# Sixteen-kilobyte rows instead of four: the expert weights of a mixture of experts, loaded one matrix at a time

## The chip, the cores and the metric

The kernel runs on one core of one Trainium2 chip. The metric is the device time of one execution in microseconds; the number of a kernel is the median of its runs. A separate execution is profiled, and its trace gives the times of single instructions and transfers.

## The reference

The computation is a small network of three layers on one sequence of 256 tokens with 1024 features, all in float32. The first two layers are a mix of a gated linear recurrence and a sparse attention; the third has an RWKV mixer beside a forgetting attention, and then a mixture of experts. Only the last part is touched here. It has 64 experts in 8 groups of 8. Each token goes to the best group, and in it to the two best experts. An expert has three matrices:

```
hid = jax.nn.silu(xblk @ w_gate[e]) * (xblk @ w_up[e])
return hid @ w_down[e]
```

Here w_gate and w_up are 1024 x 512 and w_down is 512 x 1024, so each is 2 MB, and the 64 experts hold 192 such matrices, 403 MB in all. With 256 tokens and two experts each, an expert sees few tokens, but its weights have to be read once all the same.

## The kernel before, in words

The three layers run one after the other. The weights of the first layers come through a small ring (raw, L241). The experts' weights are loaded on the SP queue into slots of 16 KB per partition, 2 MB each. There are ten at the end: some become free while the third layer's mixer still runs (L1120, L1312), the rest at its end (L1241, L1618). On the profile, some slots are called slot and three lie in the tile called arena; they take turns.

The experts run in 16 groups of four (this "group" of the kernel is half a group of the routing). For each group `experts` (L1540) does the following:

- It gathers the tokens' rows by a matmul with a selection matrix (L1534). Each expert has 32 rows, so that four experts fill 128.
- It multiplies with w_gate and w_up (L1566) into two accumulators, pg and pu. The four experts use four bands of 32 output rows (index j), and the 1024 features are summed over k = 0 to 7. A partition p holds the rows 8p to 8p+7 of an expert's matrix, so k is the row within a partition.
- Tanh on ScalarE (L1570) and two VectorE operations (L1571, L1572) make the hidden values, which PE transposes (L1576) and ScalarE copies (L1578).
- It multiplies with w_down (L1585, function `down`) into two accumulators, one for each half of the output columns, with k = 0 to 3.
- In `add` (L1588), ScalarE copies each half (L1590), a matmul weights it by the gates and puts it back in the order of the tokens (L1593), and VectorE adds it to x (L1595).

The matmuls are in float32. The trace has two matmul records for each matmul of L1566 and L1585.

`expert_load` (L1495) is the k-th of the 12 loads of a group. Loads 0 to 7 go in turn to w_gate and w_up: each takes two of the eight rows of a partition from all four experts. Loads 8 to 11 take one of the four rows of w_down from all four experts:

```
src = self.A[n][bass.ds(e0, 4)].rearrange("e (p k) f -> p e k f", k=8)[:, :, 2 * k:2 * k + 2]
```

Two rows of 512 floats lie next to each other in memory, and so does one row of 1024, so what is contiguous is 4 KB in either case, four times for each partition. Only the last group's w_down is loaded in another shape (L1501 to L1506): by halves of the columns, as two transfers for each load.

The order is set by the list `ahead` (L105) of all loads of all 16 groups. `fill` (L1515) issues the next load whenever a slot has no more readers to come in the program; `used` (L1520) says that some have been read. A load that is issued waits on the chip, on SP, until the matmuls that read its slot before have ended. What SP has behind it waits with it: later loads, and at the end the output (L1597). In `experts`, each load is given back on its own: after 16 matmul records for w_gate and w_up (eight matmuls), and also after 16 for w_down.

After the 16 groups there is a loop for experts with more than 32 rows (L1628). In the profiled execution it runs no time.

Of the kernel before, what the change touches and what calls it, by code (L numbers as in the profile page):

```python
# [11 lines left out]
OP = mybir.AluOpType  # L12
# [4 lines left out]
SLOT = 32          # rows of an expert in a pass  # L17
KEY = 512          # key of an assignment: expert * KEY + rank
# [4 lines left out]
# columns of the packed constants  # L23
# [3 lines left out]
# columns of the MoE's constants  # L27
M_KT, M_IO, M_OV, M_KG, M_END = 0, 128, 136, 144, 160
# columns of a hybrid layer's packed parameters
# [3 lines left out]
# columns of the third layer's packed parameters  # L33
# [3 lines left out]
ARENA = 24512      # floats of a partition in the one tile for what is float32 throughout  # L37
# [12 lines left out]
PAIRS = ((0, 1024, 3072), (7168, 5120, 4096))   # of a pair of chunks: where AR, M and BKt are  # L50
# [4 lines left out]
def run_all(steps):  # L55
    """Takes all steps; what they return."""
    while True:
        try:
            next(steps)
        except StopIteration as end:  # L60
            return end.value


def merged(a, b, every):
    """Steps of a, with one of b after every so many; what b returns."""
    n = 0
    for cost in a:
        yield cost
        n += 1
        if n % every == 0 and b is not None:  # L70
            try:
                yield next(b)
            except StopIteration as end:
                b, res = None, end.value
    if b is not None:
        res = yield from b
    return res


class Net:  # L80
    def __init__(self, ctx, tc, A, norm):
# [6 lines left out]
        self.holes = [(0, ARENA, 0)]        # offset, size, when freed  # L88
# [46 lines left out]
    # ---- on-chip memory: blocks whose tiles follow each other  # L135
# [9 lines left out]
    # ---- regions of one tile; Tile orders accesses to what overlaps  # L145
# [60 lines left out]
    def rot(self, shape, name, bufs=2, dt=F32, at=None):  # L206
        """The next of bufs buffers that take turns; freed by name like others."""
# [15 lines left out]
    # ---- float32 products in three passes: each operand is split exactly into two parts of 12 bits  # L223
# [8 lines left out]
    # ---- weights: blocks stream through a ring, in the order in which they are used  # L232
# [15 lines left out]
    def weights_steps(self, name, k, pin=False):  # L248
        """A weight block of k rows per partition, split."""
# [22 lines left out]
    def mm3_steps(self, out, lhs, rhs, first, last):  # L272
        """out += lhs^T rhs over lists of (hi, lo) pairs."""
# [13 lines left out]
    def rsqrt(self, out, v):  # L287
        """1 / sqrt(v) by Newton's steps, from an estimate by the exponent's bits."""
# [9 lines left out]
    # ---- h = rms_norm(x) g, rows moved to partitions (row 128 k + p), split; in steps as halves of x come  # L298
# [61 lines left out]
    def out_steps(self, yT, wo, then=None, tiles=(0, 1), half=0):  # L360
        """x += y wo, for halves of wo's rows from the given one on."""
# [25 lines left out]
    def log1p_half(self, e, z, z2, s):  # L387
        # s = log1p(e) / 2 = atanh(e / (2 + e)) for 0 <= e <= 1
# [11 lines left out]
    def hybrid_params(self):  # L400
        """Parameters of both hybrid layers; the decay constant -4 softplus(-lam)."""
# [14 lines left out]
    def chunk(self, name, pin=False):  # L416
        """A column block of an input projection: two halves of four k rows."""
        return run_all(self.chunk_steps(name, pin))
# [9 lines left out]
    def step(self, cols, pin=False):  # L428
        """Steps of the work that fills gaps, for about so many columns of the tensor engine."""
        self.pin = pin  # L430
        while cols > 0:
            n = next(self.side, None)
            if n is None:
                return
            cols -= n
# [16 lines left out]
    def hybrid(self, l, w0, then):  # L452
# [17 lines left out]
        # ---- q, k_s, k_w: token layout, norm, rotary; v_s, v_w  # L470
# [54 lines left out]
        # ---- compressed keys and values  # L525
# [7 lines left out]
        # partial sums over half of the rows each: keys at partitions 0 and 32, values at 64 and 96  # L533
        pcp = self.p("tp")
        Xs, cks = [], []
        for a in range(2):
# [11 lines left out]
            # token 16 n + 2 j + par  # L548
# [65 lines left out]
        # ---- compressed branch: scores of all heads, softmax, weights by gate  # L614
# [35 lines left out]
        # ---- selected and window branches: a head's three stages beside those of others  # L650
# [43 lines left out]
    def rg_part(self, l, hT, yT, sgn):  # L694
        """The recurrent half, in steps."""
# [17 lines left out]
        def silu(w, out):  # L713
            # without its factor 0.5
# [33 lines left out]
        # u = sqrt(1 - a^2) * i * x, with 1 - a^2 = tanh(-log a) (1 + a^2)  # L748
# [16 lines left out]
    def softmax(self, ps, mask, gate, at=None):  # L765
        """Weights of a head's scores [128 q, (q tile 0: 128 keys, q tile 1: 256)]."""
# [19 lines left out]
    def turned(self, P):  # L786
        """Keys moved to partitions."""
# [23 lines left out]
    def mixer(self, w0, more):  # L811
# [8 lines left out]
        # what the chunks' products read, by pairs of chunks: each pair's room becomes one slot of the experts' weights  # L820
        AR = [self.t([128, 4, 2, 2, 64], f"AR{i}", at=a[0]) for i, a in enumerate(PAIRS)]    # m, parity, (alpha, rho), t
        BK = self.t([128, 4, 2, 2, 2, 64], "BK")    # m, pair, parity, (kappa, beta) or (beta, kappa), s
        UV = self.t([128, 2, 2, 8, 64], "UV")       # v, and what the chunks add, with tokens on partitions
# [30 lines left out]
        # tanh of the decay rows; the rows of a stay as they are; sigmoid of the gate rows  # L854
# [17 lines left out]
        # log decay, its running sum within chunks of 64, P = exp of it  # L872
# [13 lines left out]
        # k: unit vectors kk (per head), k' = k (1 + (a - 1) k_a)  # L886
# [7 lines left out]
        def rest(w2):  # L894
            # r, v and the attention's q and k, between the steps of the inverse
# [66 lines left out]
        # a = 0.5 (1 + ta); beta = kk a / P; kappa = k' / P; alpha = -kk P_{t-1}; rho = r P  # L962
# [13 lines left out]
        # (I - B)^-1 for the strictly upper B[s, t] = beta_s . alpha_t: blocks of 1, 2, 4, 8, 16 merged within  # L976
        # blocks of 32, then those; partitions: even chunks at 64, odd ones at 0
        B = self.t([128, 2, 8, 64], "B", at=4608)
        BT, Q, BO = (self.t([128, 2, 8, 32], n, at=a) for n, a in (("BT", 10240), ("Q", 6656), ("BO", 10752)))
        TX = self.t([128, 2, 2, 8, 32], "TX", at=5632)      # the inverse and its transpose  # L980
# [96 lines left out]
        # products within chunks: rows (kappa, beta), columns (alpha, rho)  # L1077
# [15 lines left out]
        # the chunks in order: U = T (alpha S + A_ak V), Y = rho S + [A_rk A_rb] [V U], S = (S + [kappa beta] [V U]) P  # L1093
# [3 lines left out]
        # what the group norm multiplies and adds: weight, bonus and shift, each by the gate  # L1097
# [25 lines left out]
        def norm(i, y):  # L1123
            # group norm, bonus, gate
# [29 lines left out]
        def parts():  # L1154
            # of the output projection what the heads and the first tokens allow
# [14 lines left out]
        def other():  # L1170
            """Some of what is beside the chain."""
# [77 lines left out]
    def fox_gate(self, z):  # L1249
        T, V, S = self.T, self.V, self.S  # L1250
        c = self.c
        # -cumsum of log sigmoid(z), in three parts that bf16 carries exactly
# [5 lines left out]
        V.scalar_tensor_tensor(s, s, 2.0, e, OP.mult, OP.subtract)      # -log f  # L1258
# [20 lines left out]
    def fox_qk(self, hT, wi):  # L1279
        """q and k of the attention, to be taken in small steps between other work."""  # L1280
# [34 lines left out]
    def fox_heads(self, v, yT, more):  # L1315
        """The heads' attention in stages, a head's three beside those of others."""
# [35 lines left out]
    # ---- routing: top 1 of 8 groups, top 2 of its 8 experts  # L1352
    def route_init(self):
# [9 lines left out]
        self.oh = t([128, 2, 3, 8], "r_oh")             # tile; group, choices  # L1363
# [7 lines left out]
        self.key = t([128, 2, 2], "r_key")              # choice, tile  # L1371
# [7 lines left out]
    def route_step(self, tt, hf):  # L1379
        """Half a token tile of x is final."""  # L1380
# [14 lines left out]
        if hf:  # L1395
            if tt:
                # the first experts' rows among the first tile's, while the second tile is routed
# [4 lines left out]
    def route_tile(self, tt):  # L1402
# [16 lines left out]
        def first(vals, top, i):  # L1419
            # index - 128 and one-hot of the first of vals that equals top  # L1420
# [12 lines left out]
        # el holds the logits with their sign turned  # L1433
# [7 lines left out]
        # one-hot of both over the 64 experts; an assignment's rank among its expert's  # L1441
# [16 lines left out]
        # keys as group g of four experts sees them  # L1458
        V.tensor_tensor(self.keyg[:, :, :, tt], self.key[:, :, tt].unsqueeze(1).broadcast_to([128, 16, 2]),
                        self.cm[:, M_KG:M_KG + 16].unsqueeze(2).broadcast_to([128, 16, 2]), OP.subtract)  # L1460
        # the two choices' probabilities
# [10 lines left out]
    def route_more(self):  # L1472
        """Passes beyond the first: how many multiples of SLOT the fullest expert exceeds."""
# [9 lines left out]
    # ---- experts  # L1483
    first = None

    def moe_memory(self):
        """Room for what the routing and the experts need; the rest in slots for 2 MB of weights each."""
# [6 lines left out]

    def expert_load(self, g, k):  # L1495
        """The k-th of the 12 loads of four experts' weights."""
        e0, n, k = g * 4, "wd" if k > 7 else ("wg", "wu")[k % 2], k - 8 if k > 7 else k // 2
        w = self.slots[self.nslot % len(self.slots)]
        self.nslot += 1
        if n == "wd" and isinstance(g, int) and g == 15:  # L1500
            # the last: columns by halves  # L1501
# [5 lines left out]
        if n == "wd":  # L1507
            src = self.A[n][bass.ds(e0, 4)].rearrange("e (p k) d -> p e k d", k=4)[:, :, k:k + 1]
        else:
            src = self.A[n][bass.ds(e0, 4)].rearrange("e (p k) f -> p e k f", k=8)[:, :, 2 * k:2 * k + 2]  # L1510
# [4 lines left out]
    def fill(self):  # L1515
        """Loads of what is next into the slots that have no more readers to come."""
# [7 lines left out]
    def gather(self, key, kt):  # L1524
        """Rows of x for four experts, transposed, in a step for each token tile."""
# [14 lines left out]
    def experts(self, key, kt, out=None):  # L1540
        """Four experts: their rows of this pass gathered, run, and added into x by gate."""
# [19 lines left out]
        for k2 in range(0, 8, 2):  # L1561
            for dst in (pg, pu):
                w = self.early.pop(0)
                for k in (k2, k2 + 1):
                    for j in range(4):
# [250 lines left out]
```

## Time and profile before

| | us |
|---|---|
| median of three runs | 1565.11 |
| lowest and highest run | 1561.07, 1567.47 |
| span of the profiled execution | 1561.9 |
| PE busy | 1200.3 |
| VectorE busy | 545.6 |
| ScalarE busy | 309.1 |

The span goes from the first to the last instruction. PE's busy time counts matmuls whose ends are modelled and that overlap each other, so it is not a measure of PE at its peak. In the page's 40 slices a slice is 39 us; the digit is the busy share in tenths. The experts begin at about 600 us, slice 15. The line of DMA gives the mean share of the 16 DMA engines, and GB/s what they moved. A share may come out slightly above 1, as packets overlap a little at their ends. A "packet" of the page is what a DMA engine moves in one piece.

### The profile page before, as it was taken

To read this page: it belongs to the slowest core of one execution; us is meant where nothing else is said; L and a number is where in the kernel's file an instruction comes from. 1 tells how busy PE (TensorE), PEld (TensorE's weight loads), DVE (VectorE), ACT (ScalarE), POOL (GpSimd) and SP (SyncE) were. 2 spreads that over 40 slices of the span, in tenths; PEclk is the share of its full clock that TensorE was granted. 3 is DMA by queue.
4 is the path that set the end of the run, shared out by engine and by line. 5 is a ranking of instruction groups with operands and counts; after the bars stand their busy time and mean duration, and the time that the engine had idled before them with its cause. 6 is when DMAs were issued, how large, how long until landed. Compare 5 with 4: busy or idle time off the path is not lost.

```text
span 1561.9 us, 20735 instructions
## 1 busy us (share of the span) xinstructions
PE 1200.3 (77%) x8695; PEld 664.4 (43%) x8695; DVE 545.6 (35%) x1380; ACT 309.1 (20%) x733; POOL 170.9 (11%) x156
## 2 busy tenths in 40 slices
PE   6799989988889998887685775766766756758765
PEld 5767777767767674333132230331331312313311
DVE  6968786777665464111010110110101101101001
ACT  4556455644323221000000000000000000000000
POOL 3412431244232200000000000000000000000000
PEclk9999989998997798887788788997888989888888
DMA  7421532232311268999999999999999999999996
GB/s 273 161 96 41 213 128 97 79 140 92 111 57 54 108 250 343 409 409 410 409 409 409 410 409 409 410 409 409 409 409 409 409 409 409 409 409 409 409 408 254
DMA packets 113412, 464.94 MB, mean 298 GB/s; under 512 B 4236, under 2 KB 4364, under 8 KB 107428
## 3 DMA queue, kind: packets, MB, share of 16 engines
q1 hardware_dynamic: 113316, 463.58, 75.6%
q8 instruction: 70, 1.15, 0.3%
q14 instruction: 26, 0.21, 0.0%
HBM read 462.51 MB, written 1.05 MB: 297 GB/s over the span
## 4 chain that ended last, share of the span: by engine, by line
DMA 46%; PE 25%; DVE 5%; ACT 1%; issue 1%; POOL 0%; ACTq 0%; DVEq 0%
DMA slot<-in_wu 18%; DMA slot<-in_wg 13%; DMA arena<-in_wg 9%; PE sc L1566 5%; PE tp L1534 5%; DMA arena<-in_wu 5%; PE mm L277 5%; PE ot L1585 3%; DMA slot<-in_wd 1%; DVE w L261 1%; PE tp L1576 1%; DVE arena L1572 1%; PE sc L1083 1%; PE ot L1026 1%; PE sc L1329 0%
## 5 line engine op out<-in xcount | busy, mean ns | idle before, releaser
L1566 PE MATMUL sc<-slot,arena 128*32 128x512 f32 x1424 | 229.9, 780 | 167.0 <-DMA slot<-in_wu 104.0
L1566 PEld LDWEIGHTS sc<-slot,arena 128*32 128x32 f32 x1424 | 44.4, 128 | 344.7 <-DMA slot<-in_wu 161.4
L1571 DVE SCALAR_TENSOR_TENSOR arena<-arena,sc 128x512 f32<-128x512 f32 x16 | 11.0, 687 | 486.2 <-ACT arena L1570 486.2
L261 POOL TENSOR_TENSOR w<-raw,w 128x512 fp32r<-128x512 f32 (+2 forms) x100 | 138.2, 1400 | 260.9 <-ACT w L258 184.6
L1566 PE MATMUL sc<-arena 128*32 128x512 f32 x624 | 102.0, 788 | 72.4 <-DMA arena<-in_wg 46.8
L277 PE MATMUL mm<-hT,w 128*128 128x256 f32 (+1 forms) x936 | 138.9, 301 | 3.1 <-DVE arena L840 1.9
L1534 PEld LDWEIGHTS tp<-arena 128*128 128x128 f32 x512 | 124.4, 334 | 20.1 <-issue 20.1
L1534 PE MATMUL tp<-arena 128*128 128x128 f32 x512 | 129.1, 408 | 2.4 <-DVE arena L1532 2.4
L277 PEld LDWEIGHTS mm<-hT,w 128*128 128x128 f32 (+1 forms) x936 | 123.4, 199 | 15.8 <-issue 8.9
L1585 PE MATMUL ot<-slot,arena 128*32 128x512 f32 x720 | 94.8, 652 | 28.2 <-DMA slot<-in_wd 27.4
L277 PE MATMUL mm<-w,hT 128*128 128x512 f32 (+1 forms) x432 | 105.6, 396 | 6.4 <-DVE w L261 3.0
L258 ACT CAST w<-raw 128x512 fp32r<-128x512 f32 (+2 forms) x182 | 97.6, 594 | 39.8 <-PE mm L277 22.7
L1570 ACT ACTIVATE arena<-sc 128x512 f32<-128x512 f32 x16 | 9.6, 597 | 481.5 <-PE sc L1566 481.5
L261 DVE TENSOR_TENSOR w<-raw,w 128x512 fp32r<-128x512 f32 (+2 forms) x100 | 90.6, 927 | 9.3 <-ACT w L258 9.2
L1595 DVE TENSOR_TENSOR arena<-arena,mm 128x512 f32<-128x512 f32 x64 | 44.0, 687 | 135.5 <-PE mm L1593 135.5
L277 PEld LDWEIGHTS mm<-w,hT 128*128 128x128 f32 x432 | 78.4, 199 | 22.8 <-DVE w L261 3.9
L1566 PEld LDWEIGHTS sc<-arena 128*32 128x32 f32 x624 | 19.5, 129 | 151.1 <-DMA arena<-in_wg 72.3
L277 PE MATMUL mm<-w,y 128*128 128x512 f32 x288 | 75.3, 404 | 0.8 <-DVE y L225 0.8
L1590 ACT COPY arena<-ot 128x512 f32<-128x512 f32 x32 | 18.7, 585 | 268.8 <-PE ot L1585 268.8
L1593 PE MATMUL mm<-arena 128*128 128x512 f32 x128 | 68.3, 660 | 1.6 <-ACT arena L1590 1.4
L277 PEld LDWEIGHTS mm<-w,y 128*128 128x128 f32 x288 | 52.3, 188 | 13.6 <-issue 1.9
L1585 PEld LDWEIGHTS ot<-slot,arena 128*32 128x32 f32 x720 | 20.3, 114 | 81.1 <-DMA slot<-in_wd 42.9
(392 smaller groups left out, 1247.8 us busy)
## 6 DMA issues: line engine op xcount, KB each, us to landing
slot<-in_wu SPq DMA_DIRECT2D x51, 2048.0 KB, 23.8
slot<-in_wd SPq DMA_DIRECT2D x42, 2048.0 KB, 23.8
slot<-in_wg SPq DMA_DIRECT2D x38, 2048.0 KB, 23.9
arena<-in_wg SPq DMA_DIRECT2D x26, 2048.0 KB, 24.0
arena<-in_wd SPq DMA_DIRECT2D x18, 2048.0 KB, 24.0
raw<-in_w_in SPq DMA_DIRECT2D x32, 1024.0 KB, 4.6
arena<-in_wu SPq DMA_DIRECT2D x13, 2048.0 KB, 24.0
raw<-in_w_out SPq DMA_DIRECT2D x12, 1024.0 KB, 4.9
```

Of the source, the lines that this page charges most:

```text
L258: a = (self.V.tensor_copy if i in (XM if name[-1] == "2" else XH) else self.S.copy)(hi[:, sl], w[:, sl])
L261: (self.G if i < 2 else self.V).tensor_tensor(lo[:, sl], w[:, sl], hi[:, sl].bitcast(F32), OP.subtract)
L277: ins = self.T.matmul(out, lhsT=lhs[k][a], rhs=rhs[k][b], start=(first and i == 0 and k == 0), stop=(last and i == 2 and k == n - 1))
L1026: ins = T.matmul(o[qd(q, d), h * 32:(h + 1) * 32], lhsT=lhs[qd(q, d), h], rhs=rhs[qd(q, d), h], start=True, stop=True)
L1083: T.matmul(ps[:, cc * 128:(cc + 1) * 128], lhsT=BK[hb, m, cc // 2, cc % 2].rearrange("p w t -> p (w t)"), rhs=AR[cc // 2][hb, m, cc % 2].r ...
L1534: ins = T.matmul(self.rows[k // 4][:, k % 4 * 128:(k % 4 + 1) * 128], lhsT=hv[:, tt, k], rhs=D[:, tt], start=(tt == 0 and k % 4 == 0), sto ...
L1566: T.matmul(dst[32 * j:32 * j + 32], lhsT=XT[:, k, 32 * j:32 * j + 32], rhs=w[:, j, k % 2], start=(k == 0), stop=(k == 7))
L1572: V.scalar_tensor_tensor(hid, hid, 0.5, pu, OP.mult, OP.mult)
L1585: T.matmul(py[h][32 * j:32 * j + 32], lhsT=HT[:, k, 32 * j:32 * j + 32], rhs=w[:, j], start=(k == 0), stop=(k == 3))
L1590: S.copy(Y[:, cs], py[h])
L1593: T.matmul(pc, lhsT=DT[:, tt * 128:(tt + 1) * 128], rhs=Y[:, cs], start=True, stop=True)
L1595: V.tensor_tensor(xs, xs, pc, OP.add)
```

## The change

In the groups 1 to 14 a load is one expert's whole matrix. Its 128 partitions each get 8 rows (w_gate, w_up) or 4 rows (w_down) that lie next to each other in memory, 16 KB. The order of a group's 12 loads becomes four of w_gate, four of w_up, four of w_down. The bytes, the number of loads, the slots and where an element ends up by partition and row are the same. Groups 0 and 15 keep the loads from before ("fine"); so does the shape by halves of the last w_down.

The matmuls follow. In the middle groups the loop over k runs over four loads at a time, since each of the four experts' loads is needed for every k. The four slots are given back together, after 64 matmul records. For w_down the halves of the output become the outer loop. The number of matmuls is the same. The loop for experts with more than 32 rows also takes whole matrices. Comments are left out in the new file.

```diff
+    @staticmethod
+    def fine(g):
+        return isinstance(g, int) and g in (0, 15)
+
     def expert_load(self, g, k):
-        e0, n, k = g * 4, "wd" if k > 7 else ("wg", "wu")[k % 2], k - 8 if k > 7 else k // 2
+        e0 = g * 4
         w = self.slots[self.nslot % len(self.slots)]
         self.nslot += 1
-        if n == "wd" and isinstance(g, int) and g == 15:
+        if not self.fine(g):
+            n, e = ("wg", "wu", "wd")[k // 4], e0 + k % 4
+            src = self.A[n][bass.ds(e, 1)].rearrange("e (p k) f -> p (e k) f", p=128)
+            v = w.rearrange("p (k f) -> p k f", k=src.shape[1])
+            self.nc.sync.dma_start(v, src)
+            return v
+        n, k = "wd" if k > 7 else ("wg", "wu")[k % 2], k - 8 if k > 7 else k // 2
+        if n == "wd" and g == 15:
...
-    def experts(self, key, kt, out=None):
+    def experts(self, key, kt, out=None, fine=False):
...
-        for k2 in range(0, 8, 2):
+        def up(dst, k, w):
+            for j in range(4):
+                T.matmul(dst[32 * j:32 * j + 32], lhsT=XT[:, k, 32 * j:32 * j + 32], rhs=w(j), start=(k == 0),
+                         stop=(k == 7))
+        if fine:
+            for k2 in range(0, 8, 2):
+                for dst in (pg, pu):
+                    w = self.early.pop(0)
+                    for k in (k2, k2 + 1):
+                        up(dst, k, lambda j: w[:, j, k % 2])
+                    self.used(1)
+        else:
             for dst in (pg, pu):
-                w = self.early.pop(0)
-                for k in (k2, k2 + 1):
-                    for j in range(4):
-                        T.matmul(dst[32 * j:32 * j + 32], lhsT=XT[:, k, 32 * j:32 * j + 32], rhs=w[:, j, k % 2],
-                                 start=(k == 0), stop=(k == 7))
-                self.used(1)
+                w = [self.early.pop(0) for _ in range(4)]
+                for k in range(8):
+                    up(dst, k, lambda j: w[j][:, k])
+                self.used(4)
...
-        for k in range(4):
-            wd = self.early.pop(0)
+        if fine:
+            for k in range(4):
+                wd = self.early.pop(0)
+                for h in range(2):
+                    down(h, k, lambda j: wd[:, j, 0, h * 512:(h + 1) * 512])
+                self.used(1)
+        else:
+            wd = [self.early.pop(0) for _ in range(4)]
             for h in range(2):
-                down(h, k, wd[:, :, 0, h * 512:(h + 1) * 512])
-            self.used(1)
+                for k in range(4):
+                    down(h, k, lambda j: wd[j][:, k, h * 512:(h + 1) * 512])
+            self.used(4)
...
         for g in range(16):
-            self.experts(self.keyg[:, g], kt, out if g == 15 else None)
+            self.experts(self.keyg[:, g], kt, out if g == 15 else None, self.fine(g))
```

More of the change, by code (lines that the diff above doesn't have):

```diff
@@ L1507, in expert_load @@
         if n == "wd":
-            src = self.A[n][bass.ds(e0, 4)].rearrange("e (p k) d -> p e k d", k=4)[:, :, k:k + 1]
+            src = self.A[n][e0:e0 + 4].rearrange("e (p k) d -> p e k d", k=4)[:, :, k:k + 1]
         else:
-            src = self.A[n][bass.ds(e0, 4)].rearrange("e (p k) f -> p e k f", k=8)[:, :, 2 * k:2 * k + 2]
+            src = self.A[n][e0:e0 + 4].rearrange("e (p k) f -> p e k f", k=8)[:, :, 2 * k:2 * k + 2]
         v = w.rearrange("p (e k f) -> p e k f", e=4, k=src.shape[2])
@@ L1584, in down @@
             for j in range(4):
-                T.matmul(py[h][32 * j:32 * j + 32], lhsT=HT[:, k, 32 * j:32 * j + 32], rhs=w[:, j],
+                T.matmul(py[h][32 * j:32 * j + 32], lhsT=HT[:, k, 32 * j:32 * j + 32], rhs=w(j),
                          start=(k == 0), stop=(k == 3))
@@ L1602, in experts @@
                         wd = self.early.pop(0)
-                    down(h, k, wd[:, :, k % 2])
+                    down(h, k, lambda j: wd[:, j, k % 2])
                     if k % 2:
```

## Prediction

> **What bounds the kernel now.** I read the page first, then the stretches of the expert stage, then the instructions of two groups and of the tail in order of time.
>
> ```profile
> span 1561.9 us, 20735 instructions
> ...
> DMA  7421532232311268999999999999999999999996
> GB/s 273 161 96 41 213 128 97 79 140 92 111 57 54 108 250 343 409 409 410 409 409 409 410 409 409 410 409 409 409 409 409 409 409 409 409 409 409 409 408 254
> DMA packets 113412, 464.94 MB, mean 298 GB/s; under 512 B 4236, under 2 KB 4364, under 8 KB 107428
> ...
> q8 instruction: 70, 1.15, 0.3%
> q14 instruction: 26, 0.21, 0.0%
> ...
> DMA slot<-in_wu 18%; DMA slot<-in_wg 13%; DMA arena<-in_wg 9%; PE sc L1566 5%; PE tp L1534 5%; DMA arena<-in_wu 5%; PE mm L277 5%; PE ot L1585 3%; DMA slot<-in_wd 1%; DVE w L261 1%; PE tp L1576 1%; DVE arena L1572 1%; PE sc L1083 1%; PE ot L1026 1%; PE sc L1329 0%
> ```
>
> From slice 16 (about 625 us) to the end the transfers run flat at 409 GB/s, and the chain that ended last is mostly weight loads. The stage's rate, and the same columns for four short stretches used below (the last three columns are the granted clock, the DMA share and GB/s):
>
> ```profile
> core 0: us, PE busy (x) PEld busy (x) DVE busy (x) ACT busy (x) POOL busy (x), PEclk, DMA share, GB/s
> 650.00:1500.00 850.00, 583.13 (x3288) 217.82 (x3284) 103.23 (x214) 38.15 (x70) 0.00 (x0) 0.85 1.03 409
> 24.50:28.14 3.64, 3.64 (x17) 2.67 (x15) 3.20 (x14) 2.23 (x5) 1.21 (x2) 1.00 1.01 432
> 182.00:185.00 3.00, 3.00 (x15) 2.49 (x14) 3.00 (x3) 2.58 (x6) 3.00 (x2) 1.00 1.01 431
> 181.00:185.00 4.00, 4.00 (x19) 3.33 (x18) 3.48 (x3) 3.58 (x7) 4.00 (x3) 1.00 0.98 418
> 569.00:574.00 5.00, 5.00 (x24) 4.14 (x23) 4.37 (x16) 0.00 (x0) 0.00 (x0) 1.00 1.03 421
> ```
>
> In 650 to 1500 us the DMA engines are full (share 1.03) while PE is busy 583 of 850 us. So a 2 MB load (2,097,152 bytes) costs 2097/409 = 5.13 us. PE shows the same pace from the other side, in the last group:
>
> ```profile
> 1512.63 1.92 PE L1566 MATMUL sc<-slot,arena 128*32 128x512 f32 x16 [1.53 <-DMA slot<-in_wg]
> 1517.74 3.60 PE L1566 MATMUL sc<-slot,arena 128*32 128x512 f32 x16 [3.19 <-DMA slot<-in_wu]
> 1522.87 1.92 PE L1566 MATMUL sc<-slot,arena 128*32 128x512 f32 x16 [1.53 <-DMA slot<-in_wg]
> ...
> 1528.00 3.59 PE L1566 MATMUL sc<-slot,arena 128*32 128x512 f32 x16 [3.20 <-DMA slot<-in_wu]
> ...
> 1549.24 1.94 PE L1585 MATMUL ot<-slot,arena 128*32 128x512 f32 x8 [1.50 <-DMA slot<-in_wd]
> ```
>
> Each load's matmuls start when it lands, (1528.00 - 1512.63)/3 = 5.12 us apart. I use 5.12. The last ones start at 1549.24, 12.7 us before the end.
>
> **The change, part by part.** Its main effect is the length of a row in one transfer. Before, a load is 128 partitions times 4 experts of 4 KB; after, 128 rows of 16 KB. The question is whether the engines move 16 KB rows faster than 4 KB rows. The kernel already has one such transfer, in_w_cmp, twice:
>
> ```profile
> raw<-in_w_in SPq DMA_DIRECT2D x32, 1024.0 KB, 4.6
> ...
> raw<-in_w_out SPq DMA_DIRECT2D x12, 1024.0 KB, 4.9
> ...
> arena<-in_w_cmp SPq DMA_DIRECT2D x2, 2048.0 KB, 8.4
> ```
>
> 2048 KB over 128 partitions is 16 KB in a row. First, does such a row stay whole? The page counts 113412 - 107428 = 5984 packets of 8 KB or more. The in_w_in and in_w_out loads of 1024 KB give (32 + 12) x 128 = 5632 rows of 8 KB; the instruction queues 70 + 26 = 96; two in_w_cmp loads of 128 rows give 256. The sum is 5984: a row is one packet. Cut at 8 KB, the in_w_cmp rows would have made 512.
>
> Second, its rate: the windows in which in_w_cmp flows show 432 (24.50 to 28.14) and 431 GB/s (182 to 185), with the engines as full (1.01) as later. They are short, and one load deep. The same 4 KB loads show 421 in a short stretch (569 to 574) and 409 in the long one, so long streams lose something. Three ways to carry that over:
> - No loss for long rows: 2097/432 = 4.85 us a load.
> - Loss per packet: 16 engines x 4096 B / 409 = 160.2 ns a packet against 155.7 at 421, 4.5 ns each. A 16 KB packet at 432 is 606.8 ns; 611.3 with the loss, 429 GB/s, 4.89 us.
> - Loss per byte: 432 x 409/421 = 420 GB/s, 5.00 us.
>
> I take the middle, 4.89 us, because a price per packet also explains most of the distance from 432 to 421 in the short stretches. The Trainium skill ("DMA: Bandwidth & Descriptors", section "Why small descriptors are slow (HBM only)") puts the fixed cost at about 3 cycles per packet, on beats of 32 B. With its 850 MHz an estimate by that page is 154.1 ns for 4 KB and 605.9 ns for 16 KB, which would save 0.085 us a load, 14 us in all. The trace agrees on 16 KB and disagrees on 4 KB (160.2 ns).
>
> The count: groups 1 to 14 have 12 loads each, 168. All are issued in the full stretch, as the issue queue shows:
>
> ```profile
> 608.72 0.37 SPq L1512 DMA_DIRECT2D arena<-in_wd  x1
> 610.44 0.37 SPq L1512 DMA_DIRECT2D slot<-in_wd  x1
> 612.18 0.37 SPq L1512 DMA_DIRECT2D arena<-in_wg  x1
> ```
>
> The two wd loads are the last of group 0, the wg at 612.18 the first of group 1. So the term is 168 x (5.12 - 4.89) = 38.6, about 39 us; ends 168 x 0.12 = 20 and 168 x 0.27 = 45 us.
>
> Next, slots. The ten slots are freed four at a time, after 64 matmul records instead of 16. What must hold: after the fourth load of a batch has landed, six further slots cover 6 x 4.89 = 29.3 us. A landing without a queue takes 7.6 us at least, 2.5 more than its 5.12 us of bytes:
>
> ```profile
> DMA to landing us min/median/max: 7.6/23.9/25.3
> ```
>
> So a batch must be read and released within P = 29.3 - 2.5, about 27 us. The work in between, and what delays it:
>
> ```profile
> 613.63 7.05 PE L1566 MATMUL sc<-slot,arena 128*32 128x512 f32 x64
> ```
>
> ```profile
> 720.07 3.64 PE L1566 MATMUL sc<-arena 128*32 128x512 f32 x16 [2.08 <-DMA arena<-in_wg]
> ...
> 730.23 2.05 PE L1534 MATMUL tp<-arena 128*128 128x128 f32 x8
> ...
> 734.06 5.98 PE L1534 MATMUL tp<-arena 128*128 128x128 f32 x24
> ...
> 747.48 3.95 PE L1593 MATMUL mm<-arena 128*128 128x512 f32 x8
> ```
>
> A batch of 64 takes 7.05 us when PE runs through, 4 x 3.64 = 14.6 us at the slow pace of one that has just waited. For wu, P is 7 to 15 us. For wd it is about the same: its input has the 19.6 us of four loads to get ready. For wg the end of the group before stands in front: down 7.05 to 14.6, add 3.95, gather 2.05 + 5.98 = 8.0, so 19.0 to 26.6 us after wd landed, while wg lands 19.6 us after it. P is 7 to 7.0 + 14.6 = 21.6 us. Cost zero, cover 5 us at the worst.
>
> Edits at nothing: the number of matmuls, additions and issues stays (12 loads a group); that all of wg comes ahead of wu, and each half of the output in one go, moves PE's work within a stage that PE does not bound. Each load's issue now makes 128 packets instead of 512; on SP only later loads and the output stand behind it. PE waiting for the fourth load costs nothing where DMA sets the pace; at the hand-over to group 15, up to 19 us of backlog meet eight fine loads, 41 us, with 1.92 to 3.64 us of matmuls each, and are gone before the last. Group 15 and its tail of 12.7 us are as before. The Trainium skill ("Perfetto Trace Analysis", section "DMA Optimizations") advises smaller transfers where engines idle, so that work starts sooner; the trace does not meet that condition, share 1.03.
>
> **Sum.** The profiled span goes from 1561.9 to 1561.9 - 39 = 1523 us. The three runs' median, 1565.11, is 3.2 above that span; minus 39 it gives 1526 us.
>
> **Rivals.**
> - Long streams lose by byte, or the short windows read too high. For it: 181 to 185 shows 418 GB/s, the long stream's loss is seen with one size only, and its cause not at all. Against it: two windows at 431 and 432. At 418 a load is 5.02 us, 168 x 0.10 = 17 us saved; at 420, 20. Time about 1546. The page's 3 cycles, above, come out beside it at 1551.
> - No effect: the transfer is still made of short packets, or 409 is the limit of a full ten-slot stream whatever its rows. Against it: the packet count, and 432. Time 1565.
> - Slower: the batch hand-over starves the queue at wg. PE is in order, and slots are sometimes handed on late, by an instruction behind the reader:
>
> ```profile
> SPq L1512 <- PE sc L1566: 164.5, 94, 18.7
> SPq L1512 <- PE ot L1585: 123.6, 29, 6.4
> SPq L1512 <- PE mm L1593: 63.9, 15, 4.9
> SPq L1512 <- PE tp L1534: 46.6, 11, 6.0
> ```
>
> Here 15 waits ended with the add (L1593), after wd was read. It begins at P = 27; each us beyond costs 14 us, one for each group. At 29.8 it eats the 39 us, at 30.4 it is 8 us slower than before. At P = 32 the time is 1526 + 5 x 14 = 1596. Against it: my worst P is 21.6, and the mean clock of 0.85 says that PE is seldom at its slow pace for long; a longer run of matmuls meets fewer of the waits before it.
>
> **How the numbers follow.** The forecast (over 20 and up to 45 us saved, likeliest 39): 0.75. First rival: 0.12. No effect: 0.06. Slower: 0.07. A measurement here can tell about 0.5%, 8 us, from no change. Faster by more: 0.75 + 0.12 = 0.87, less 0.01 for a small effect, 0.86; same 0.07; slower 0.07. The range reaches from 45 us saved less 2 us of spread, 1518, past the first rival to the page's 1551, cut to 1549: it leaves out the last two cases and a little, under 0.2.
>
> **What would show it.** Right: from about 625 to 1485 us a flat GB/s near 429 (420 to 432), DMA share still about 1; packets under 8 KB fewer by 168 x 512 = 86016; the last group's loads still 5.12 us apart; DMA still the chain. Wrong: 409 with long rows (no effect); slices below 420 with a DMA share under 1 and issue waits that end at L1566's successors or at the add (starved); or PE taking over the chain.

## The result, and the profile after

The changed kernel takes 1528.32 us in the median of six runs (1524.94 to 1536.75), the kernel before 1566.07 us beside it (six runs, 1561.07 to 1572.37). The ratio is 0.9758, with a 95% interval of 0.972 to 0.9795. The forecast was 1526 us.

The page of the profile after (its line of slices and what stands below it):

```profile
span 1535.0 us, 20733 instructions
...
DMA  7430542234122149899999999999999999999996
GB/s 278 142 120 29 176 171 84 76 102 165 58 85 64 40 150 385 355 427 427 429 428 426 429 428 428 426 428 427 427 428 427 428 427 428 427 428 428 424 408 253
DMA packets 48900, 464.94 MB, mean 303 GB/s; under 512 B 4236, under 2 KB 4364, under 8 KB 21412
...
PE 39%; DMA 32%; DVE 5%; issue 2%; ACT 1%; POOL 0%; ACTq 0%; DVEq 0%
```

The flat stretch now stands at 426 to 429 GB/s where it stood at 408 to 410, up to the last group, whose loads are the old ones (408). The packets below 8 KB are fewer by 107428 - 21412 = 86016, which is 168 x 512, and those of 8 KB or more have become more by (48900 - 21412) - 5984 = 21504, which is 168 x 128: every load of the middle groups now goes in 128 packets of 16 KB. The stretch in one row (the last three columns are the granted clock, the DMA share and GB/s), and the first 100 us for comparison:

```profile
0.00:100.00 100.00, 78.26 (x459) 65.56 (x460) 74.15 (x180) 44.27 (x104) 35.43 (x41) 0.90 0.53 191
...
650.00:1450.00 800.00, 607.68 (x3227) 233.30 (x3226) 100.55 (x210) 36.38 (x67) 0.00 (x0) 0.85 1.01 428
```

The DMA engines are full as before (share 1.01, before 1.03). The profiled execution itself is one of the longer ones (1535.0 us of span). Its first layers, which the change does not touch, run 10.4 us later than in the profile before: the first slot of the experts is handed back at 619.10 us instead of 608.72.

```profile
619.10 0.37 SPq L1525 DMA_DIRECT2D arena<-in_wd  x1
620.82 0.37 SPq L1525 DMA_DIRECT2D slot<-in_wd  x1
622.56 2.03 SPq L1510 DMA_DIRECT2D arena<-in_wg  x2
```

In the same first 100 us the profile before has a granted clock of 0.97, this one 0.90:

```profile
0.00:100.00 100.00, 77.51 (x490) 64.78 (x490) 77.74 (x198) 47.80 (x116) 35.73 (x42) 0.97 0.52 196
```

Whether that is why the first layers took longer is not shown. Either way the two spans should not be subtracted as they stand. From the first returned slot to the end it was 1561.9 - 608.72 = 953.2 us and is 1535.0 - 619.10 = 915.9 us: 37.3 us less, as the medians say (37.75; by the interval of the ratio 32 to 44).

The tail, PE's last matmuls in order of time:

```profile
1517.21 1.06 PE L1607 MATMUL ot<-arena 128*32 128x512 f32 x8 [0.58 <-DMA arena<-in_wd]
1519.76 1.07 PE L1607 MATMUL ot<-slot,arena 128*32 128x512 f32 x8 [1.48 <-DMA slot<-in_wd]
1522.32 1.94 PE L1607 MATMUL ot<-slot,arena 128*32 128x512 f32 x8 [1.50 <-DMA slot<-in_wd]
```

The last of them starts 1535.0 - 1522.32 = 12.7 us before the end, as before.

### The profile page after: what moved, and what is told of

The parts are those of the page before. It is cut to its first block, busy times and chain, and to the rows that moved or that the text cites. A ratio compares the mean times of both kernels' runs of the same rounds, so it can differ in the third digit from the quotient of the medians.

```text
span 1535.0 us, 20733 instructions
## 1 busy us (share of the span) xinstructions
PE 1246.9 (81%) x8695; PEld 695.5 (45%) x8695; DVE 545.7 (36%) x1380; ACT 309.1 (20%) x733; POOL 171.1 (11%) x156
## 2 busy tenths in 40 slices
DMA packets 48900, 464.94 MB, mean 303 GB/s; under 512 B 4236, under 2 KB 4364, under 8 KB 21412
## 4 chain that ended last, share of the span: by engine, by line
PE 39%; DMA 32%; DVE 5%; issue 2%; ACT 1%; POOL 0%; ACTq 0%; DVEq 0%
DMA slot<-in_wu 24%; PE sc L1576 10%; PE ot L1607 8%; PE tp L1547 8%; DMA arena<-in_wu 6%; PE mm L277 5%; DMA slot<-in_wd 1%; PE tp L1598 1%; DVE w L261 1%; DVE arena L1594 1%; PE ot L1026 1%; PE sc L1083 1%; PE mm L1615 0%; PE sc L1329 0%; PE ot L1195 0%
## 5 line engine op out<-in xcount | busy, mean ns | idle before, releaser
L1576 PE MATMUL sc<-slot,arena 128*32 128x512 f32 x1424 | 322.1, 736 | 139.7 <-DMA slot<-in_wu 83.3
L1576 PE MATMUL sc<-arena 128*32 128x512 f32 x624 | 191.1, 740 | 54.6 <-DMA arena<-in_wu 37.1
L1576 PEld LDWEIGHTS sc<-slot,arena 128*32 128x32 f32 x1424 | 71.8, 131 | 353.9 <-issue 154.7
L277 PE MATMUL mm<-hT,w 128*128 128x256 f32 (+1 forms) x936 | 144.3, 309 | 2.5 <-DVE arena L840 1.1
L277 PEld LDWEIGHTS mm<-hT,w 128*128 128x128 f32 (+1 forms) x936 | 127.7, 206 | 16.9 <-issue 10.0
L1547 PEld LDWEIGHTS tp<-arena 128*128 128x128 f32 x512 | 124.4, 334 | 18.8 <-issue 18.8
L1607 PE MATMUL ot<-slot,arena 128*32 128x512 f32 x720 | 127.9, 601 | 5.7 <-DMA slot<-in_wd 5.0
L1547 PE MATMUL tp<-arena 128*128 128x128 f32 x512 | 128.9, 407 | 2.4 <-DVE arena L1545 2.4
L1594 DVE SCALAR_TENSOR_TENSOR arena<-arena,sc 128x512 f32<-128x512 f32 x16 | 11.0, 688 | 267.6 <-PE sc L1576 267.6
L1593 DVE SCALAR_TENSOR_TENSOR arena<-arena,sc 128x512 f32<-128x512 f32 x16 | 11.0, 688 | 263.1 <-ACT arena L1592 263.1
L1576 PEld LDWEIGHTS sc<-arena 128*32 128x32 f32 x624 | 40.2, 130 | 118.1 <-DMA arena<-in_wu 51.0
L1600 ACT COPY arena<-tp 128x512 f32<-128x512 f32 x16 | 9.4, 585 | 304.5 <-PE tp L1598 304.5
L1612 ACT COPY arena<-ot 128x512 f32<-128x512 f32 x32 | 18.7, 585 | 250.8 <-PE ot L1607 250.8
L1607 PE MATMUL ot<-arena 128*32 128x512 f32 x304 | 67.0, 597 | 0.6 <-DMA arena<-in_wd 0.6
```

Of the source, the lines that this page charges most:

```text
L277: ins = self.T.matmul(out, lhsT=lhs[k][a], rhs=rhs[k][b], start=(first and i == 0 and k == 0), stop=(last and i == 2 and k == n - 1))
L1547: ins = T.matmul(self.rows[k // 4][:, k % 4 * 128:(k % 4 + 1) * 128], lhsT=hv[:, tt, k], rhs=D[:, tt], start=(tt == 0 and k % 4 == 0), sto ...
L1576: T.matmul(dst[32 * j:32 * j + 32], lhsT=XT[:, k, 32 * j:32 * j + 32], rhs=w(j), start=(k == 0), stop=(k == 7))
L1594: V.scalar_tensor_tensor(hid, hid, 0.5, pu, OP.mult, OP.mult)
L1607: T.matmul(py[h][32 * j:32 * j + 32], lhsT=HT[:, k, 32 * j:32 * j + 32], rhs=w(j), start=(k == 0), stop=(k == 3))
L1612: S.copy(Y[:, cs], py[h])
```

## The experiments

Three theories were held against each other. A: only the length of a packet counts, each packet having a fixed price. B: the gain comes from the new order of the work, with matmuls in batches, slots handed back by four, and memory read one matrix at a time. C: there are two rates, one for rows up to 4 KB and another above. Two more kernels test the step on the slots.

**e1_whole_4k.** The changed kernel, with pieces of 4 KB. Each row of 16 KB is written in pieces that do not follow each other in the slot, so that it cannot be one packet; the matmuls find the pieces where they lie (that part of the edit is left out here).

```diff
...
-            self.nc.sync.dma_start(v, src)
+            src = src.rearrange("p (a c x) -> p a c x", a=2, c=2)
+            v = w.rearrange("p (c a x) -> p a c x", a=2, c=2)
+            for a in range(2):
+                self.nc.sync.dma_start(v[:, a], src[:, a])
...
```

> As the changed kernel, one expert's matrix at a time, read in the same batches of four, but its 16 KB rows are placed as four pieces of 4 KB in another order, two transfers of 1 MB a load, so that a packet is 4 KB. Theory A (the gain is the length of the packet): the rate falls back to 409 GB/s, 5.12 us a load, and the time to that of before, 1566 us (1558 to 1574). Theory B (the gain is the order of the work: PE's matmuls in batches of 64, slots handed back by four, one stretch of memory read at a time): the time stays at 1528 us with 428 GB/s.

Measured: 1565.74 us, ratio to before 1.0014 (0.9986 to 1.0041). The flat stretch:

```profile
650.00:1450.00 800.00, 594.66 (x3076) 233.97 (x3074) 97.77 (x206) 35.47 (x65) 0.00 (x0) 0.85 1.03 409
```

```profile
DMA packets 116102, 464.97 MB, mean 297 GB/s; under 512 B 6924, under 2 KB 7052, under 8 KB 110116
```

The pieces are packets of 4 KB: of those under 8 KB there are 110116 - 21412 = 88704 more than in the changed kernel, which is 168 x 512 and 16 short ones for each of the 168 added transfers (under 512 B, 6924 - 4236 = 2688). All of the gain is gone, on engines as full as before (1.03), although the order of the work and the batches are those of the change. Theory B falls. So does a rival that was not named, that what counts is how much lies together in memory: here a transfer reads 8 KB in a row from memory and scatters it in the slot, the kernel before reads 4 KB in a row and writes 16 KB together, and both run at 409 GB/s.

**e2_whole_8k and e3_whole_2k.** The first loads each matrix as two transfers with 8 KB in a row, and everything stays in its place; the second is e1_whole_4k with c=4, pieces of 2 KB.

> As the changed kernel, but each matrix in two transfers of 1 MB, 8 KB in a row. Theory A, with a fixed price for each packet: 160.2 ns for 4 KB and 16 engines x 16384 B / 428 GB/s = 612.5 ns for 16 KB make 36.8 ps a byte and 9.4 ns a packet, so 8 KB takes 310.9 ns, 421 GB/s, 4.97 us a load, 168 x 0.15 = 25 us less than before: 1541 us. Theory B: 1528 us. Theory C (two rates, one for rows up to 4 KB and one above it): 1528 us or 1566 us, not between.

> As e1_whole_4k, with pieces of 2 KB. Theory A: 9.4 + 2048 x 0.0368 = 84.8 ns a packet, 386 GB/s, 5.43 us a load, 168 x 0.31 = 52 us more than before: 1618 us. Theory C: 2 KB pieces run as 4 KB pieces do, as the last transfers of the kernel before seem to, which land 2.57 us apart at 1 MB each (407 GB/s): about 1570 us. Theory B: 1528 us.

Measured: 8 KB 1538.16 us, ratio 0.982 (0.9773 to 0.9867); 2 KB 1613.48 us, ratio 1.0312 (1.0258 to 1.0365). The flat stretch of the 8 KB kernel, then that of the 2 KB kernel:

```profile
650.00:1450.00 800.00, 599.21 (x3158) 233.47 (x3159) 98.90 (x208) 35.42 (x65) 0.00 (x0) 0.85 1.01 421
```

```profile
650.00:1450.00 800.00, 572.21 (x2879) 212.80 (x2877) 91.29 (x193) 33.29 (x61) 0.00 (x0) 0.83 1.05 387
```

The rates 387, 409, 421 and 428 GB/s are, for one of 16 engines, 84.7, 160.2, 311.3 and 612.5 ns for a packet of 2, 4, 8 and 16 KB. Each further 2 KB takes 75 to 76 ns on every step, so the points lie on a line of 36.8 ns per 1000 bytes and about 9.3 ns per packet. (The rates are rounded to 1 GB/s, which for 16 KB is 1.4 ns, so the price is known to about half a nanosecond.) Two rates (theory C) would have put 8 KB at one of the ends and 2 KB at the time of 4 KB. Theory A had the 8 KB time within 3 us and the 2 KB time within 5 us.

**e2_pairs_8k.** The whole-matrix series has two transfers a load. Here 8 KB rows come in one, half of the rows of two experts (the matmuls' part of the edit is left out):

```diff
-            n, e = ("wg", "wu", "wd")[k // 4], e0 + k % 4
+            n, e = ("wg", "wu", "wd")[k // 4], e0 + k % 4 // 2 * 2
+            m = 2 if n == "wd" else 4
-            src = self.A[n][bass.ds(e, 1)].rearrange("e (p k) f -> p (e k) f", p=128)
+            src = self.A[n][bass.ds(e, 2)].rearrange("e (p k) f -> p e k f", p=128)[:, :, k % 2 * m:k % 2 * m + m]
...
```

> 8 KB in a row again, but one transfer a load as in both kernels: half of the rows of two experts. It parts the length of the packet from the number of transfers, which e2_whole_8k doubled. Theory A: 421 GB/s and 1538 us, as e2_whole_8k measured. If the second transfer of a load had cost something of its own, this is faster than that, up to the 1528 us of the changed kernel.

Measured: 1540.54 us, ratio 0.9836 (0.9794 to 0.9878), and in the flat stretch the same rate to the digit:

```profile
650.00:1450.00 800.00, 560.82 (x3176) 219.73 (x3170) 98.42 (x207) 36.02 (x66) 0.00 (x0) 0.85 1.01 421
```

The number of transfers, 1 MB or 2 MB each, makes no difference that can be measured; nor does it matter whether one matrix or two are read at a time.

The two kernels also settle a rival that was not named. The change shortens the time for which an issue occupies SP, from 4.87 us in the median to 0.38 (shown in the last section), and one could take that for the cause. At 8 KB the pairs have the long issues and the two halves the short ones (the issues of w_up, first in e2_pairs_8k, then in e2_whole_8k; least, median and greatest time in ns), at the same 421 GB/s:

```profile
L1511 SPq DMA_DIRECT2D slot<-in_wu x38: 368/4579/6832, 622.5 to 1413.6; - x38
```

```profile
L1512 SPq DMA_DIRECT2D slot<-in_wu x76: 327/328/328, 624.7 to 1422.7; - x76
```

**e4_7_slots and e4_6_slots.** From group 2 on, the loads use a smaller ring, whose places are the last m slots of the old one in their order:

```diff
+            if g == 2:
+                n, m = self.nslot, 7
+                self.slots = [self.slots[(i - m) % 10] for i in sorted(range(n, n + m), key=lambda i: i % m)]
```

> As the changed kernel, but from group 2 on the loads take turns in 7 slots instead of 10. This tests the step on the hand-over of slots. In the profile of the changed kernel a batch is read 7 to 9 us after its fourth load lands. If that is so throughout, three slots cover 3 x 4.9 - 2.5 = 12.2 us and nothing is lost: 1528 us. If the prediction's worst case for wg (21.6 us) is what PE needs, the queue runs dry for 9.4 us in each of 13 groups, 122 us: 1650 us.

> As e4_7_slots, with 6 slots from group 2 on. Two slots are left beside a batch: 2 x 4.9 - 2.5 = 7.3 us of cover for the 7 to 9 us in which the profile of the changed kernel reads a batch. If those figures hold, the queue runs dry for up to 1.7 us in each of 39 batches: between 1528 and 1594 us, with waits on SP that end at the matmuls and a DMA share under 1. If a batch were given back earlier than its last matmul, nothing is lost: 1528 us.

Measured: 7 slots 1528.28 us, ratio 0.9764 (0.9717 to 0.9811); 6 slots 1586.56 us, ratio 1.013 (1.0091 to 1.0169). Seven cost nothing that can be measured (427 GB/s, share 1.01), six cost everything that the change had won and more. The flat stretch with 6 slots has engines that run empty at times, share 0.96:

```profile
650.00:1450.00 800.00, 591.16 (x3039) 230.23 (x3032) 94.95 (x202) 34.46 (x63) 0.00 (x0) 0.84 0.96 400
```

One batch of w_up in that kernel: on PE its fourth load and its last matmuls (the first view), on SP the issues (the second).

```profile
913.84 1.07 PE L1576 MATMUL sc<-slot,arena 128*32 128x512 f32 x3 [2.95 <-DMA slot<-in_wu]
...
921.68 1.02 PE L1576 MATMUL sc<-slot,arena 128*32 128x512 f32 x2
```

```profile
902.18 1.29 SPq L1510 DMA_DIRECT2D arena<-in_wd  x2
921.89 0.80 SPq L1510 DMA_DIRECT2D slot<-in_wd  x2
```

After the two issues at 902.18 nothing goes out until 921.89. The fourth load is there at 913.84, the last matmuls start at 921.68 and the next loads go out at 921.89: a batch is given back 8.1 us after it is complete, by its own last matmuls. Two slots cover 7.3 us of that by the sum above, an estimate. Relative to the kernel before in each comparison, 6 slots lost 18.7 us where the change gained 37.75, 56.5 in all, 1.45 us for each of 39 batches: as if a batch took 8.8 us. The 2.5 us to land in that sum were not tried by themselves.

**e7_all_up.** What is left to win this way: whole matrices in group 0 too, and for w_gate and w_up of group 15, with the matmuls in batches to match (left out here).

```diff
-        if not self.fine(g):
+        if not self.fine(g) or g == 0 or k < 8:
...
```

> As the changed kernel, with whole matrices also in group 0 and for w_gate and w_up of group 15; only the last w_down stays by halves. Theory A: ten of these loads run in the full stretch, two of group 0 and eight of group 15, 10 x 0.23 = 2.3 us less, 1526 us, which is about what a measurement can tell; unless the last w_up, whose 64 matmuls now wait for its fourth load, is late for the last w_down, which would show as a longer stretch from the last landing to the end.

Measured: 1531.44 us, ratio 0.9768 (0.9733 to 0.9803), the same as the changed kernel. Its last w_up batch and the matmuls after it:

```profile
1497.55 9.11 PE L1576 MATMUL sc<-slot,arena 128*32 128x512 f32 x58 [3.05 <-DMA slot<-in_wu]
1507.44 0.75 PE L1598 MATMUL tp<-arena 128*128 128x128 f32 x4 [0.78 <-DVE arena L1594]
1508.92 3.64 PE L1607 MATMUL ot<-slot,arena 128*32 128x512 f32 x32 [0.73 <-ACT arena L1600]
...
1518.78 1.06 PE L1607 MATMUL ot<-slot,arena 128*32 128x512 f32 x8 [0.81 <-DMA slot<-in_wd]
```

The batch is late (w_down's first 32 records find their loads there already), but PE has caught up before the last landing, for which it waits 0.81 us, and from there to the end it is 1529.4 - 1518.78 = 10.6 us, not longer than the 12.7 of the changed kernel. The expected 2.3 us are below what these runs can tell.

## Why the prediction was right

**The rate.** The step from the short windows (432 GB/s) to the long stream by a loss per packet gave 429 GB/s and 4.89 us a load; 428 GB/s and 2097/428 = 4.90 us came out. The three choices (no loss, loss per packet, loss per byte) would have given 45, 39 and 20 us; 168 x (5.12 - 4.90) = 37 us is what the term measured. The loss itself came to 612.5 - 606.8 = 5.7 ns for a packet of 16 KB where 4.5 was taken; a loss per byte would have made it about 17. That rows of 16 KB stay whole was read from the count of packets and held to the packet. What the prediction left open, whether the price belongs to the packet at all, is now shown by four lengths. Some luck was in it: the choice among the three rested on windows of 3 to 5 us, one of which read 418 (its DMA share was 0.98, so the engines were not quite full), and why a long stream loses anything was not known then and is not now.

**A rule of the Trainium skill.** By the Trainium skill ("DMA: Bandwidth & Descriptors", section "Why small descriptors are slow (HBM only)") a packet costs about 3 cycles, at its 850 MHz an estimate of 3.5 ns, by which the change would have saved 14 us. The trace does not agree in size: 9.3 ns a packet, some 8 such cycles. It agrees that the price is fixed.

**The slots.** "Cost zero" was right, but its bounds were wide: P was put at 7 to 21.6 us. Two w_up batches of the changed kernel and what PE does after the first, from the chain of waits:

```profile
1026.26 8.82 PE sc L1576 x58
...
1036.59 1.89 PE tp L1547 x8
1038.48 1.85 PE ot L1607 x8
1040.33 5.91 PE tp L1547 x24
...
1046.46 6.62 PE ot L1607 x55
1053.08 32.41 DMA arena<-in_wu
1085.54 9.89 PE sc L1576 x58
```

The w_gate batch between them, on PE from its fourth load on:

```profile
1065.96 9.00 PE L1576 MATMUL sc<-slot,arena 128*32 128x512 f32 x57 [2.97 <-DMA slot<-in_wg]
```

A batch takes 7 to 10 us, between the 7.05 of a PE that runs through and the 14.6 of the slow pace: in the w_up batch at 1026.26 the granted clock is 0.50 up to about 1029.6 and 1.00 after that. The backlog at w_gate that made up the worst case does not come: w_up was complete at 1026.26, so w_down is at about 1026.3 + 4 x 4.9 = 1045.9, and by then the gathering for the next group (L1547) is all but over and the first of the down products (L1607) are done. The prediction had set the 8.0 us of gathering behind w_down's landing; they run while w_down is still on its way. So PE is waiting when the fourth load of w_gate lands at 1065.96, as it is in each of the groups 2 to 14. With 27 us allowed, the slower rival was far away. The runs with fewer slots show that it exists and where it begins: three slots beside a batch are enough, two are not.

**Edits at nothing.** All held: the tail is 12.7 us, the matmuls of the last w_gate and w_up loads start at 1485.75, 1490.86, 1495.98 and 1501.12, still 5.12 us apart, and the busy share of PE in the flat stretch rose from 583/850 = 0.69 to 608/800 = 0.76 without a cost, as the DMA engines set the pace.

**A sign that failed.** The prediction asked for "DMA still the chain" and named PE taking over the chain as a sign of being wrong. The chain now says PE 39%, DMA 32%, and yet DMA bounds: the rate of the packets explains each of the times, and with 7 slots the chain has PE at 44% and DMA at 27% for the same 1528 us. The lines above show how it comes about: the load of w_up in the chain lands 32.41 us after its issue, more than six loads of 4.9, so it stands in the queue behind others. The chain goes back from it to the matmuls that gave its slot back and counts them as PE, while the engines are kept full by the loads ahead. The DMA share (1.01), not the chain, was the right sign.

## What to carry to other kernels

Where the DMA share stands at 1 for hundreds of microseconds, compute bytes per engine and packet from its GB/s: if packets are short, longer contiguous rows are worth their fixed price, here 9.3 ns each (4 KB to 16 KB: 409 to 428 GB/s); a transfer in the same trace that already has the longer row tells the rate beforehand, in a window in which the engines are full. When loads then have to be read in batches, count the slots left beside a batch, times the time of a load, less the time to land: that must exceed the time to read a batch, and one slot too few costs more than the longer rows gain.

## What the runs showed of the hardware

- The time per packet lies on one line from 2 to 16 KB, with a fixed price of about 9.3 ns: 387, 409, 421 and 428 GB/s on full engines.
- A long stream runs a little below a short one: 409 against 421 for 4 KB, 428 against 432 for 16 KB. Why was not tried. The last transfers of the kernel, 1 MB each in rows of 2 KB, land 2.56 us apart (1517.21, 1519.76, 1522.32), 410 GB/s, faster than the 387 of a long stream of such rows; that too is open.
- With 512 packets of 4 KB an issue occupied SP for 4.87 us in the median, about the time of a load, as if it had to wait for room behind the loads before it; that reason is not shown. With 128 packets of 16 KB it takes 0.38 us, and SP waits for the slots instead. It is not the length of the packet alone: 256 packets of 8 KB in one transfer took 4.58 us, 128 of them 0.33. The lines of w_up before and after, with the least, the median and the greatest time in ns:

```profile
L1512 SPq DMA_DIRECT2D slot<-in_wu x51: 368/4869/5656, 523.3 to 1503.8; - x51
```

```profile
L1510 SPq DMA_DIRECT2D slot<-in_wu x38: 327/382/1330, 629.4 to 1408.1; - x38
```
